# A hybrid encoder block on one core: the order of query splits, key splits, gate sums and refill steps

## The chip, the cores and the metric

The kernel runs on one core of a Trainium2 chip. The metric is the device time of one execution in microseconds (us), as the median of several executions. A profile of one execution shows every instruction of the core's engines: TensorE (PE, matmuls; PEld its weight loads), VectorE (DVE), ScalarE (ACT), GpSimd (POOL) and SyncE (SP, which here only issues DMA transfers). Each engine works through its own instructions in order, and an instruction that waits for another engine or for a transfer holds back everything behind it on its engine.

## What is computed

One encoder block on a sequence of 1024 rows of width 1024 with 16 learned rows put ahead, all in float32:

```python
u = _rms_norm(h, pre_w)
z = u @ w_in
rq, rk, rv, rg, aq, ak, av, ag, gr, ga = _split_in(z)
# branch A: two-way retention of rotary rq, rk with rv, 4 heads, chunks of 128
o_r = o_r * ret_nw * silu(rg)
y_r = o_r @ w_rb
# branch B: attention in a window of +-128 rows, 8 query heads in 2 groups,
# with the 16 learned rows always seen, and a sink in the softmax
o_a = o_a * silu(ag)
y_a = o_a @ w_ab
mix = sigmoid(gr) * y_r + sigmoid(ga) * y_a
return h + _rms_norm(mix @ w_o, post_w)
```

## The kernel before

**Numbers in two halves.** Every float32 operand of a large matmul is split into an upper part `h`, its value in the matmul's own format, and a lower part `l = x - h`. ACT (sometimes POOL) makes the upper part by a copy, and DVE the lower one by a subtraction (`dve_lo`, L92). A product is then three matmuls (`mm3`, L76 to L78): upper by upper, lower by upper, upper by lower. So nearly every operand passes through ACT and then DVE before PE can use it, and PE asks for the lower part one matmul after the upper one.

**Stages.** First the retention heads (to about 330 us), with projections run in between; then attention (about 330 to 549 us); then four phases of large products: `z` (the gates, from about 545 us), `r`, `a` (the two branches) and `o` (the output).

**Attention** (`attention`, from L1410) goes through 32 chunks, four pairs of heads with eight blocks of 128 queries. A chunk has three steps: `stage1` computes scores `ps` (PE), DVE adds the mask and takes the extremes (L1447, `raw`, `nm`), ACT takes exponentials (L1450); `stage2` transposes the scaled weights (PE, `pt`, L1483 to L1488) and splits them into `pah`/`pal`, `pbh`/`pbl` and `pm` (ACT, DVE); `stage3` multiplies with the values (PE, `po`). The banks of `pt` are used in turn, so PE can transpose for the next chunk only when DVE has read the last one. Between these steps PE does projections, in *steps* of three matmuls: `fill(n)` runs n steps. The table `BEGUN` (L1575 on) says which side tasks are written behind which step: fetching and splitting weights (`fetch_aq`, `half_w`), splitting queries (`split_q`, L670: ACT makes `aqh` in L678, DVE `aql`) and keys (`keys`, L717: ACT `kTh` in L724, DVE `kTl`), sums for later phases (`sum_row`, `pre_sum`, `pre_parts`). `hooked` (L848) ties each of these tasks behind the last exponential, row sum and softmax parts that were written ahead of it. Queries and keys are rotated in `rope_late` (L183): two DVE products (L187, L188), and two DMAs issued by POOL that add the turned halves (L192). The rotated tile can be split when these have landed.

**Start of attention.** `gen_av` (L903) projects the values, nine blocks; the last one's product `pav` is evacuated by ACT (`vah`, L917) and DVE (`val`, L918). Before the change this is done ahead of the first lines of `attention`; the first chunk's queries are split inside its own `stage1`.

**The phases.** Each phase is done in units `u` of seven products `p` of half-size blocks (a Strassen-like scheme), so that operands are sums and differences of blocks (`Phase.prepare`, L991). Units come in pairs: the order in phase `z` starts (0,1), (1,1), (0,3), (1,3), (0,2), (1,2), written as (unit, product). `run` prepares six products ahead (`LEAD = 6`). For the first two units of `z` (`early`) product 3 needs A12 - (A21 + A22 - A11), three DVE steps (L1025 to L1027) on tile `st`, then its split into `lhz` (ACT, L987) and `llz` (DVE). `Phase.split` notes its lower part in the list `ahead`: it always holds the lower part written last. Partial results gather in PSUM banks; `combine` (L1068) copies one to `u3` (ACT) and adds another to it (DVE, L1077), which frees that bank for the next product.

**Refills.** The right-hand blocks `B11`, `T1`, `B21`, `B22` lie in tiles `big`. While a phase ends, `refill` (L1154) writes the next phase's blocks into them: it loads pieces (SP), copies the upper part (ACT, L963) and subtracts the lower part (DVE, L92, `big<-a`). It gives each step a place counted from the phase's last product: -7 is seven products before. Phase `a`'s refill, for `o`, is the last and the shortest; its T blocks come ready made from DRAM.

**What sets the order.** The program's order is not the order of the queues. When the kernel is built, a planner with cost estimates of its own orders every engine's instructions by their place in the program and by when it expects their inputs. `tc.issue_after(i)`, and `follow(...)` around it, forbids one thing: instructions inside that run on the same engine as `i` may not be put ahead of `i`. They tie nothing on other engines.

Of the kernel before, what the change touches and what calls it, by code (L numbers as in the profile page):

```python
# [18 lines left out]
NB = SEQ // P  # L19
# [20 lines left out]
def block_kernel(ctx: ExitStack, tc: tile.TileContext, x0, xT, x, meta, w_in, w_rb, w_ab, w_out, post_w,  # L40
                 rope, tab, out):
    nc = tc.nc
# [232 lines left out]
    with tc.tile_pool(name="setup", bufs=1, reuse_waits="tile") as st:  # L275
# [61 lines left out]
        for k in range(KT):  # L337
            t = xr[k]
# [24 lines left out]
        split, wv0 = halves_w(U_V)  # L363
# [18 lines left out]
        first = [projT(wv0, 0, "pv0_0", vmeta0), projT(wv0, 1, "pv0_1"), projT(wv0, 2, "pv0_2")]  # L382
# [287 lines left out]
    def split_q(hp, e_, i):  # L670

        o = aq[hp][e_, i].rearrange("p (t q) -> p t q", q=64)
        if (hp, i) not in aqs:
            aqs[hp, i] = [aw.tile([P, 1024], R, tag=f"aq{t}", bufs=2, name=f"aq{t}{hp}_{i}") for t in "hl"], set()
            if len(aqs) == 1:
                aw.tile([P, 48], F32, name="space_aq")
        h, l = (t.rearrange("p (t e q) -> p t e q", e=2, q=64)[:, :, e_] for t in aqs[hp, i][0])
        nc.scalar.copy(h, o)  # L678
        dve_lo(l, o, h)
        aqs[hp, i][1].add(e_)  # L680


    def fetch_aq(hp):
# [219 lines left out]
    def gen_av():  # L903
        w = load_w(w_in, U_AV)
        for c in range(9):
            mt = None if c else vmt
            t = projT(w, c, f"pav{c}", mt)
            if c == 0:
                nc.scalar.activation(mt, mt, AF.Copy, scale=rcol[0:NM, 0:1])

                for r in range(4):
                    nc.vector.tensor_copy(vm[32 * r:32 * r + NM], mt)
                dve_lo(mt.bitcast(R), mt, vm[0:NM])
                for r in range(2):
                    nc.sync.dma_start(vm[32 * r + NM:32 * r + 2 * NM].bitcast(F32), mt)
            else:
                nc.scalar.activation(vah[:, c - 1], t[:, 0:256], AF.Copy, scale=rcol[:, c:c + 1])  # L917
                nc.vector.scalar_tensor_tensor(low_value(c - 1), t[:, 0:256], rcol[:, c:c + 1],  # L918
                                               vah[:, c - 1].bitcast(F32), op0=ALU.mult, op1=ALU.subtract)
            if NB - 3 < c < NB:  # L920
                yield


    av = gen_av()
# [41 lines left out]
    class Phase:  # L966
# [18 lines left out]
        def split(self, u, p, src):  # L985
            h, l = (lp.tile([P, 4, P], R, tag=t, bufs=LEAD, name=f"{t}{self.nm}{u}_{p}") for t in ("lh", "ll"))
            nc.scalar.copy(h, src)  # L987
            ahead[:] = [dve_lo(l, src, h)]
            self.ops[u, p] = h, l

        def prepare(self, u, p):  # L991
            if self.cur is not None and u // 2 != self.cur:
                self.raw = {}
            self.cur = u // 2
            g = nc.vector.tensor_tensor
            made = {1: 2, 6: 3}.get(p)
            if made not in self.pre.get(u, ()):
                made = None
            for q in (p, made):
                if self.fetch and q in POST and u not in self.early:  # L1000
                    self.fetch(u, *POST[q])
            if made:
                self.e[u, made] = gtile(f"e{u}{made}")
                nc.sync.dma_start(self.e[u, made], e_d[u, made])
            if p in (1, 2, 4):
                self.split(u, p, self.block(u, PROD[p][0]))
            elif p == 7:
                t = lp.tile([P, 4, P], F32, tag="st", bufs=3, name=f"st{self.nm}{u}S3")
                g(t, self.block(u, "A11"), self.block(u, "A21"), sub)
                self.split(u, 7, t)  # L1010
            elif p == 5:
                t = self.s[u] = lp.tile([P, 4, P], F32, tag="st", bufs=3, name=f"st{self.nm}{u}S")
                g(t, self.block(u, "A21"), self.block(u, "A22"), add)
                self.split(u, 5, t)
                g(t, t, self.block(u, "A11"), sub)
            elif p == 6:
                t = self.s[u]
                self.split(u, 6, t)
                if u in self.early or 3 in self.pre.get(u, ()):
                    del self.s[u]  # L1020
                else:
                    g(t, self.block(u, "A12"), t, sub)
            elif u in self.early:
                t = lp.tile([P, 4, P], F32, tag="st", bufs=3, name=f"st{self.nm}{u}S4")
                g(t, self.block(u, "A21"), self.block(u, "A22"), add)  # L1025
                g(t, t, self.block(u, "A11"), sub)
                g(t, self.block(u, "A12"), t, sub)  # L1027
                self.split(u, 3, t)
            else:
                self.split(u, 3, self.s.pop(u))  # L1030
# [123 lines left out]
    def refill(nm, src):  # L1154

        x = {}

        def load(i, j, ks=range(4)):
            def f():
                for k in ks:  # L1160
                    x[i, j, k] = t = stage(f"{nm}{i}{j}{k}", j)
                    src(t, 4 * i + k, j)
            return f

        def minus(o, a, b):
# [12 lines left out]
        def step(at, n, f):  # L1178
            for k, j in enumerate(n):
                at.setdefault(j, []).append(lambda k=k: f(k))  # L1180

        if nm == "a":
            at = {-16: [load(0, 0)], -14: [load(1, 1)]}
            each(at, -13, split("B11", 0, 0))
            at.update({-11: [got("T1")], -10: [load(1, 0)], -9: [got("T2")], -5: [got("T3")], -1: [got("T4")]})
            each(at, -7, split("B21", 1, 0))
            each(at, -3, split("B22", 1, 1))
            return at

        first = -21 if nm == "z" else -17  # L1190
        at = {first: [load(0, 0), load(0, 1)], -13: [load(1, 1)], -9: [load(1, 0, range(3))]}
        def behind(f):
            def g(k):
                with tc.issue_after(ahead[0]):
                    f(k)
            return g

        step(at, range(first + 2, first + 6), behind(minus((0, 1), (0, 1), (0, 0))))
        step(at, (-13, -12, -11, -10), split("B11", 0, 0))
        step(at, (-11, -10, -9, -8), split("T1", 0, 1))  # L1200
        step(at, (-9, -8, -7, -6), minus((0, 1), (1, 1), (0, 1)))
        step(at, (-7, -6, -5, -4), split("T2", 0, 1))
        step(at, (-5, -4, -3, -2), minus((0, 0), (0, 1), (0, 0)))
        step(at, (-3, -2, -1, 3), split("B21", 1, 0))
        step(at, (-1, 0, 1, 3), minus((0, 1), (1, 0), (0, 1)))
        at[0].append(load(1, 0, (3,)))
        step(at, (0, 1, 2, 4), behind(split("T3", 0, 0)))
        step(at, (4, 5, 6, 7), behind(split("B22", 1, 1)))
        step(at, (7, 8, 9, 10), behind(split("T4", 0, 1)))
        return at  # L1210
# [199 lines left out]
    def attention():  # L1410
# [123 lines left out]
                 gen_aq(3, 0), gen_aq(3, 1), pre]  # L1534
        fill = filler([hooked(works, BEGUN)])[0]

        with follow(*latest):
            fill(3)
        with follow(*latest):
            stage1(0, 0)  # L1540
        for k, (hp, n) in enumerate(chunks):
# [28 lines left out]
            if k in (12, 14, 21):  # L1570
# [13 lines left out]
             76: [(sum_row, 3, 1)], 79: [(sum_fetch, 4)], 82: [(split_q, 2, 0, 0)], 88: [(sum_row, 4, 0)],  # L1584
             89: [(sum_row, 4, 1)], 90: [(split_q, 2, 1, 0)], 92: [(sum_fetch, 5)], 100: [(sum_row, 5, 0)],
             101: [(sum_row, 5, 1)], 102: [(fetch_aq, 3)], 104: [(keys, 1, 1)], 105: [(sum_fetch, 6)],
             110: [(split_q, 2, 0, 1)], 116: [(keys, 1, 2)], 117: [(half_w, 'q', 3, 0)], 121: [(half_w, 'q', 3, 1)],
             122: [(pre_fetch, 9)], 123: [(sum_row, 6, 0)], 124: [(sum_row, 6, 1)], 126: [(split_q, 2, 1, 1)],
             127: [(sum_fetch, 7)], 133: [(pre_sum, 9, 0)], 134: [(pre_sum, 9, 1)], 136: [(keys, 1, 3)],
             139: [(pre_sum, 9, 2)], 140: [(pre_parts, 9)], 141: [(pre_fetch, 10)], 145: [(split_q, 3, 0, 0)],  # L1590
             146: [(sum_row, 7, 0)], 147: [(sum_row, 7, 1)], 150: [(split_q, 3, 1, 0)], 152: [(pre_sum, 10, 0)],
             153: [(pre_sum, 10, 1)], 155: [(pre_sum, 10, 2)], 157: [(pre_parts, 10)], 158: [(pre_fetch, 11)],
             164: [(split_q, 3, 0, 1)], 166: [(pre_sum, 11, 0)], 167: [(pre_sum, 11, 1)], 168: [(pre_sum, 11, 2)],
             170: [(pre_parts, 11)], 171: [(pre_fetch, 12)], 172: [(split_q, 3, 1, 1)], 176: [(pre_sum, 12, 0)],
             178: [(pre_sum, 12, 1)], 179: [(pre_sum, 12, 2)], 181: [(pre_parts, 12)], 182: [(pre_fetch, 13)],
             187: [(pre_sum, 13, 0)], 188: [(pre_sum, 13, 1)], 189: [(pre_sum, 13, 2)], 190: [(pre_parts, 13)]}

# [112 lines left out]
```

## Time and profile before

| | |
|---|---|
| median of 3 runs | 1034.35 us (1034.12 to 1037.31) |
| profiled execution | 1035.83 us |
| its span, first to last instruction | 1034.1 us |
| granted PE clock | 0.998 |
| instructions | 17322 |
| DMA | 188.45 MB, mean 182 GB/s |
| PE at work until / span | about 1027 / 1034.1 us |

The rows of the profile that the prediction shows are read thus. In the timeline, a row is one instruction: its start from the span's start, its length, engine, line, operation, the tile it writes and those it reads, shape, and in brackets the time that its engine stood idle before it and what ended that. Buffer numbers are left out of tile names. In the list of waits a row tells who waited for whom, the total in us, how often, and the longest. In the table of stretches, each row gives the stretch and its length, each engine's busy time in it, the granted clock, the share of time in which the DMA engines were busy, and GB/s.

### The profile page before, as it was taken

Reading aid. Unit: us, or ns where it says so; the run is one execution under the profiler, and the core shown is the slowest. Engines: PE = TensorE matmul, PEld = TensorE weight load, DVE = VectorE, ACT = ScalarE, POOL = GpSimd, SP = SyncE. Lnnn points to the kernel's source line nnn. Section 1 sums busy time; section 2 is a strip of 40 time slices with the busy share of each in tenths; the row PEclk is TensorE's granted clock in tenths of the full one; section 3 lists DMA queues with packets and bytes.
Section 4 is the critical chain, followed back from the end, with each engine's and each line's share of the span. In section 5 each row is a group of like instructions: output and inputs, shape, how many; then the busy total and the mean of one; then the engine's idle time right before and its main releaser. Section 6 shows DMA issues by size and latency. Waiting matters only on the chain. (4 is left out here: it accounts for less than half of the span.)

```text
span 1034.1 us, 17322 instructions
## 1 busy us (share of the span) xinstructions
PE 1022.3 (99%) x5883; PEld 898.8 (87%) x5883; DVE 831.9 (80%) x1802; ACT 502.0 (49%) x1129; POOL 226.3 (22%) x368
## 2 busy tenths in 40 slices
PE   9999999999999999999999999999999999999997
PEld 8998999989989888988888888888888888887886
DVE  7886759758876787777769999998989899777765
ACT  5531432523423466655667555455567456333442
POOL 3445244243341424443310000000000000110032
PEclk9999999999999999999999999999999999999999
DMA  9433123243241447666559589899874756889563
GB/s 360 164 87 88 63 46 87 76 78 112 80 97 62 103 152 206 184 183 174 154 171 347 178 287 330 312 319 319 276 265 141 257 196 200 246 216 330 139 122 81
DMA packets 98840, 188.45 MB, mean 182 GB/s; under 512 B 13024, under 2 KB 37632, under 8 KB 98192
## 3 DMA queue, kind: packets, MB, share of 16 engines
q1 hardware_dynamic: 81200, 162.89, 46.6%
q0 software_dynamic: 10176, 14.73, 9.5%
q10 hardware_dynamic: 7376, 9.73, 2.8%
q8 instruction: 46, 0.75, 0.3%
q14 instruction: 42, 0.34, 0.1%
HBM read 124.32 MB, written 57.68 MB: 176 GB/s over the span
## 5 line engine op out<-in xcount | busy, mean ns | idle before, releaser
L1310 POOL DMA_DIRECT2D mx_d<-c1a x4 | 3.6, 891 | 395.3 <-DMA a<-in_w_out_dram 368.6
L77 PE MATMUL bz<-big,llz 128*128 128x512 f32 x192 | 74.9, 390 | 0.5 <-DVE llz L92 0.5
L78 PE MATMUL bz<-big,lhz 128*128 128x512 f32 x192 | 74.4, 389 | 0.0
L76 PE MATMUL bz<-big,lhz 128*128 128x512 f32 x192 | 74.1, 389 | 0.0
L76 PE MATMUL pv<-wh,big 128*128 128x256 f32 x256 | 72.9, 285 | 0.0
L77 PE MATMUL pv<-wh,big 128*128 128x256 f32 x256 | 72.8, 284 | 0.0
L78 PE MATMUL pv<-wl,big 128*128 128x256 f32 x256 | 72.7, 284 | 0.0
L78 PE MATMUL bz<-T,lhz 128*128 128x512 f32 x176 | 68.5, 389 | 0.0
L77 PE MATMUL bz<-T,llz 128*128 128x512 f32 x176 | 68.5, 389 | 0.0
L76 PE MATMUL bz<-T,lhz 128*128 128x512 f32 x176 | 68.2, 389 | 0.0
L1450 ACT ACTIVATE p<-raw,nm 128x337 f32<-128x337 f32 (+1 forms) x64 | 35.5, 557 | 34.1 <-DVE nm L1447 30.5
L76 PE MATMUL paq<-big,wh 128*128 128x512 f32 x128 | 51.6, 403 | 0.0
L1463 POOL TENSOR_SCALAR p<-p,den 128x336 f32<-128x336 f32 (+2 forms) x60 | 32.6, 565 | 85.9 <-DVE den L1454 81.1
L78 PE MATMUL paq<-big,wh 128*128 128x512 f32 x128 | 50.2, 392 | 0.0
L77 PE MATMUL paq<-big,wl 128*128 128x512 f32 x128 | 50.2, 392 | 0.0
L76 PEld LDWEIGHTS pv<-wh,big 128*128 128x128 f32 x256 | 48.4, 189 | 0.4
L77 PEld LDWEIGHTS pv<-wh,big 128*128 128x128 f32 x256 | 48.3, 189 | 0.4
L78 PEld LDWEIGHTS pv<-wl,big 128*128 128x128 f32 x256 | 48.3, 189 | 0.3
L92 DVE TENSOR_TENSOR wl<-wr,wh 128x1024 fp32r<-128x1024 f32 x28 | 35.1, 1258 | 11.3 <-POOL wh L89 6.7
L77 PEld LDWEIGHTS bz<-big,llz 128*128 128x128 f32 x192 | 36.1, 188 | 8.1 <-DVE llz L92 0.8
L78 PEld LDWEIGHTS bz<-big,lhz 128*128 128x128 f32 x192 | 36.0, 188 | 7.5
L76 PEld LDWEIGHTS bz<-big,lhz 128*128 128x128 f32 x192 | 36.1, 188 | 7.5
(621 smaller groups left out, 3591.2 us busy)
## 6 DMA issues: line engine op xcount, KB each, us to landing
wrz<-in_w_in_dram SPq DMA_DIRECT2D x32, 512.0 KB, 6.0
wr<-in_w_in_dram SPq DMA_DIRECT2D x29, 512.0 KB, 4.0
we<-in_w_in_dram SPq DMA_DIRECT2D x16, 512.0 KB, 4.2
tg<-tg_d SPq DMA_DIRECT2D x32, 256.0 KB, 5.3
e<-e ACTq DMA_DIRECT2D x20, 256.0 KB, 2.4
e<-e SPq DMA_DIRECT2D x20, 256.0 KB, 4.6
xn<-in_x_dram SPq DMA_DIRECT2D x8, 512.0 KB, 9.4
oTr_d<-ost SPq DMA_DIRECT2D x16, 256.0 KB, 2.1
```

The costliest lines, as they stand in the source:

```text
L76: nc.tensor.matmul(o, ah, bh, start=first, stop=False, **kw)
L77: nc.tensor.matmul(o, al, bh, start=False, stop=False, **kw)
L78: latest[:] = [nc.tensor.matmul(o, ah, bl, start=False, stop=last, **kw).ins]
L92: return nc.vector.tensor_tensor(o, i, hi.bitcast(F32), ALU.subtract).ins
L1310: nc.gpsimd.dma_start(d, to, accum_op=ALU.add)
L1450: last["exp"] = nc.scalar.activation(pp[:, x_, w0 - o:w0 - o + 1 + wid], r[:, 0:1 + wid], AF.Exp, scale=-1.0, bias=nm_[:, x_:x_ + 1], accu ...
L1463: nc.gpsimd.tensor_scalar(v, v, den[:, x_:x_ + 1], 1.0, op0=ALU.mult, op1=ALU.mult)
```

## The change

Five parts:

1. `gen_av` yields once more, ahead of the evacuation of the last value block. `attention` then writes the two splits of the first queries (`split_q(0, 0, 0)` and `split_q(0, 1, 0)`) first, and lets the last evacuation follow, tied on ACT behind the two upper parts. `split_q` returns its ACT instruction for this.
2. `keys(1, 2)` moves from step 116 to step 120 of `BEGUN`.
3. `split_q(3, 1, 1)` moves from step 172 to step 169, which lies in the fill of the chunk before.
4. In the first two units of phase `z`, the first of the three sums for product 3 is tied behind the lower part written last (for unit 0 that of (1,1), for unit 1 that of (0,3)).
5. In phase `a`'s refill, the splits of B11, B21 and B22 are tied behind the lower part written last, as other refills already do for some of theirs. The definition of `behind` moves up for this.

```diff
@@ split_q
-        nc.scalar.copy(h, o)
+        upper = nc.scalar.copy(h, o).ins
         dve_lo(l, o, h)
         aqs[hp, i][1].add(e_)
+        return upper
@@ gen_av
             else:
+                if c == NB:
+                    yield
                 nc.scalar.activation(vah[:, c - 1], t[:, 0:256], AF.Copy, scale=rcol[:, c:c + 1])
@@ Phase.prepare
             elif u in self.early:
                 t = lp.tile([P, 4, P], F32, tag="st", bufs=3, name=f"st{self.nm}{u}S4")
-                g(t, self.block(u, "A21"), self.block(u, "A22"), add)
+                with tc.issue_after(ahead[0]):
+                    g(t, self.block(u, "A21"), self.block(u, "A22"), add)
                 g(t, t, self.block(u, "A11"), sub)
@@ refill
+        def behind(f):
+            def g(k):
+                with tc.issue_after(ahead[0]):
+                    f(k)
+            return g
+
         if nm == "a":
             at = {-16: [load(0, 0)], -14: [load(1, 1)]}
-            each(at, -13, split("B11", 0, 0))
+            each(at, -13, behind(split("B11", 0, 0)))
             at.update({-11: [got("T1")], -10: [load(1, 0)], -9: [got("T2")], -5: [got("T3")], -1: [got("T4")]})
-            each(at, -7, split("B21", 1, 0))
-            each(at, -3, split("B22", 1, 1))
+            each(at, -7, behind(split("B21", 1, 0)))
+            each(at, -3, behind(split("B22", 1, 1)))
             return at
@@ attention
         fill = filler([hooked(works, BEGUN)])[0]
 
+        with follow(*[split_q(0, e_, 0) for e_ in range(2)]):
+            next(av, None)
         with follow(*latest):
             fill(3)
@@ BEGUN
-             110: [(split_q, 2, 0, 1)], 116: [(keys, 1, 2)], 117: [(half_w, 'q', 3, 0)], 121: [(half_w, 'q', 3, 1)],
+             110: [(split_q, 2, 0, 1)], 117: [(half_w, 'q', 3, 0)], 120: [(keys, 1, 2)], 121: [(half_w, 'q', 3, 1)],
...
-             170: [(pre_parts, 11)], 171: [(pre_fetch, 12)], 172: [(split_q, 3, 1, 1)], 176: [(pre_sum, 12, 0)],
+             169: [(split_q, 3, 1, 1)],
+             170: [(pre_parts, 11)], 171: [(pre_fetch, 12)], 176: [(pre_sum, 12, 0)],
```

More of the change, by code (lines that the diff above doesn't have):

```diff
@@ L1180, in step @@
                 at.setdefault(j, []).append(lambda k=k: f(k))
-        if nm == "a":
-            at = {-16: [load(0, 0)], -14: [load(1, 1)]}
-            each(at, -13, split("B11", 0, 0))
-            at.update({-11: [got("T1")], -10: [load(1, 0)], -9: [got("T2")], -5: [got("T3")], -1: [got("T4")]})
-            each(at, -7, split("B21", 1, 0))
-            each(at, -3, split("B22", 1, 1))
-            return at
-        first = -21 if nm == "z" else -17
-        at = {first: [load(0, 0), load(0, 1)], -13: [load(1, 1)], -9: [load(1, 0, range(3))]}
         def behind(f):
@@ L1196, in behind @@
             return g
+        if nm == "a":
+            at = {-16: [load(0, 0)], -14: [load(1, 1)]}
+            each(at, -13, behind(split("B11", 0, 0)))
+            at.update({-11: [got("T1")], -10: [load(1, 0)], -9: [got("T2")], -5: [got("T3")], -1: [got("T4")]})
+            each(at, -7, behind(split("B21", 1, 0)))
+            each(at, -3, behind(split("B22", 1, 1)))
+            return at
+        first = -21 if nm == "z" else -17
+        at = {first: [load(0, 0), load(0, 1)], -13: [load(1, 1)], -9: [load(1, 0, range(3))]}
         step(at, range(first + 2, first + 6), behind(minus((0, 1), (0, 1), (0, 0))))
```

## The prediction

> **What bounds the kernel now.** I read the page first, then the waits of TensorE (PE), then the timeline of each engine around every wait.
>
> ```profile
> PE 1022.3 (99%) x5883; PEld 898.8 (87%) x5883; DVE 831.9 (80%) x1802; ACT 502.0 (49%) x1129; POOL 226.3 (22%) x368
> ```
>
> PE sets the end: 1022.3 of 1034.1 us, and the change takes no matmul away. It can only remove places where PE stands still. The waits of PE list them (total us, times, longest):
>
> ```profile
> PE ps L77 <- DVE aql L92: 1.0, 2, 0.5
> PE ba L76 <- DVE u3a L1077: 0.6, 1, 0.6
> PE pt L1483 <- DVE pal L92: 0.5, 1, 0.5
> PE bz L77 <- DVE llz L92: 0.5, 1, 0.5
> PE pt L1487 <- DVE pbl L92: 0.4, 1, 0.4
> ```
>
> These are six stops, all released by VectorE (DVE). Idle time understates them, because matmuls overlap. The PE timeline at the stop in stage a (start, length, idle):
>
> ```profile
> 941.35 0.39 PE L78 MATMUL ba<-big,lha 128*128 128x512 f32 x1
> 941.58 0.39 PE L76 MATMUL bo<-big,lho 128*128 128x512 f32 x1
> 942.52 0.51 PE L76 MATMUL ba<-big,lha 128*128 128x512 f32 x1 [0.56 <-DVE u3a L1077]
> 942.86 0.40 PE L77 MATMUL ba<-big,lla 128*128 128x512 f32 x1
> ```
>
> Matmuls start 0.23 apart (941.35, 941.58). The next was due at 941.81 and came at 942.52: 0.71 lost. The one behind it comes 0.34 later, not 0.23: 0.11 more. A stop thus costs its idle plus 0.16, plus 0.11 where a matmul of this kind follows. The six are worth about 0.77 + 0.77 (ps), 0.82 (ba), 0.64 (first pt), 0.71 (bz) and 0.58 (second pt): **4.3 us, 0.4% of the time, is the ceiling**. 0.3% (3.1 us) is about what a measurement of this kernel can tell from no change.
>
> **The change part by part.** No part adds or removes work. Each changes where a step stands in its engine's in-order queue, and DVE and ScalarE (ACT) carry the prices.
>
> *First queries' splits.* ACT, then DVE, then PE, where the first scores start:
>
> ```profile
> 329.92 0.47 ACT L917 ACTIVATE vah<-pav,rcol 128x256 fp32r<-128x256 f32 x1 [1.68 <-PE pav L78]
> 330.30 1.13 ACT L678 CAST aqh<-aq 128x512 fp32r<-128x512 f32 x2
> 330.43 0.48 DVE L918 SCALAR_TENSOR_TENSOR val<-pav,rcol,vah 128x256 fp32r<-128x256 f32 x1 [1.86 <-ACT vah L917]
> 331.96 0.68 DVE L92 TENSOR_TENSOR aql<-aq,aqh 128x512 fp32r<-128x512 f32 x1
> 332.70 0.39 PE L77 MATMUL ps<-kTh,aql 128*128 128x272 f32 x1 [0.51 <-DVE aql L92]
> ```
>
> ACT idles 1.68 us for the last value product, with both query casts (1.13) queued behind it. Placed ahead, they fit into that idle time, and DVE, idle 1.86, takes the two lower parts (2 x 0.68) there. The second ends near 330.4 in place of 332.64; PE wants it at 332.04. What is late next is only the last value, 0.1 to 0.3 later, which nobody reads for several blocks. Bounds: 0.77 saved; or nothing, and the last value 1.13 later, if the query tiles' memory is not free by then. I take -0.75.
>
> *Keys, 4 steps later.* The second block of `keys(1, 2)`:
>
> ```profile
> 451.99 0.41 ACT L724 CAST kTh<-akr 128x256 fp32r<-128x256 f32 x1 [1.69 <-DMA akr<-m_ak]
> 450.33 1.22 DVE L92 TENSOR_TENSOR wl<-wr,wh 128x1024 fp32r<-128x1024 f32 x1 [0.19 <-ACT wh L118]
> 452.43 0.42 DVE L92 TENSOR_TENSOR kTl<-akr,kTh 128x256 fp32r<-128x256 f32 x1 [0.88 <-ACT kTh L724]
> 452.87 0.69 DVE L187 TENSOR_TENSOR m_aq<-paq,sr 128x512 f32<-128x512 f32 x1
> 454.07 0.56 DVE L1447 CUSTOM_DVE_ANT_0 raw<-ps,mask,nsink 128x336 f32<-128x336 f32 x1
> 456.47 0.69 DVE L92 TENSOR_TENSOR pal<-pt,pah 128x512 fp32r<-128x512 f32 x1 [0.30 <-ACT pah L1493]
> 457.87 0.42 DVE L92 TENSOR_TENSOR pbl<-pt,pbh 128x256 fp32r<-128x256 f32 x1
> ```
>
> The key cast waits 1.69 for the rotation's DMA, and DVE stands 0.88 behind it, with two rotary products (1.20 from 452.87 to 454.07) and the scores' evacuation queued. Four steps later the split is written after those products. They then run from 451.55, the key's lower part after them, and the evacuation starts 0.88 earlier, as does the chain to `pal` (end 457.16 to 456.28) and `pbl` (458.29 to 457.41). PE wanted `pal` at 456.66: the first pt stop (0.64) goes, and the second shrinks by 0.24. The keys' own readers come well over a microsecond after 453.2. The rotation's two POOL-issued DMAs for the products start earlier too. Bounds: -0.88; or nothing, if the build's ordering leaves the key split in front. I take -0.85.
>
> *Third query split, 3 steps earlier.*
>
> ```profile
> 509.64 0.42 DVE L92 TENSOR_TENSOR pbl<-pt,pbh 128x256 fp32r<-128x256 f32 x1
> 511.43 1.05 ACT L823 CAST weh<-we 128x1024 fp32r<-128x1024 f32 x1 [0.92 <-DVE we L813]
> 515.77 0.42 DVE L92 TENSOR_TENSOR pbl<-pt,pbh 128x256 fp32r<-128x256 f32 x1
> 516.12 0.68 DVE L92 TENSOR_TENSOR aql<-aq,aqh 128x512 fp32r<-128x512 f32 x1
> ```
>
> The split is tied behind the last softmax parts of its block, so it follows `pbl` at 515.77 and ends at 516.80, 0.68 after PE wants it. Three steps earlier it belongs to the block before and is tied behind the `pbl` of 509.64. ACT has 0.92 idle there for the 0.62 cast. DVE's 0.60 then delays one evacuation and one lower part that PE wants microseconds later. I take -0.77; the other end, +0.3, is that evacuation's chain becoming late.
>
> *First gate sums.* Each of the first two units forms A21+A22-A11 and A12 minus that (L1025, L1026, L1027):
>
> ```profile
> 544.32 0.69 DVE L1025 TENSOR_TENSOR stz0S<-wrz,wrz 128x512 f32<-128x512 f32 x1 [3.66 <-DMA wrz<-in_w_in_dram]
> 545.04 0.69 DVE L1026 TENSOR_TENSOR stz0S<-stz0S,wrz 128x512 f32<-128x512 f32 x1
> 545.65 0.68 DVE L92 TENSOR_TENSOR llz<-wrz,lhz 128x512 fp32r<-128x512 f32 x1
> 544.51 0.62 ACT L987 CAST lhz<-wrz 128x512 fp32r<-128x512 f32 x1
> 549.40 0.68 DVE L1025 TENSOR_TENSOR stz1S<-wrz,wrz 128x512 f32<-128x512 f32 x1
> 554.82 0.68 DVE L92 TENSOR_TENSOR llz<-stz1S,lhz 128x512 fp32r<-128x512 f32 x1
> 556.00 0.39 PE L77 MATMUL bz<-big,llz 128*128 128x512 f32 x1
> ```
>
> Two sums stand before the lower part that PE waits for. Behind it, `llz` starts when its cast ends, 545.16 instead of 545.65: 0.49 of the 0.71 goes, 0.1 to 0.2 stays. But unit 0's sums now also wait for the second `llz` (unit 1), and unit 1's first sum for unit 0's third lower part. By my count that part ends at 550.8 (three sums and a cast of 0.62 after about 547.6), so unit 1's chain starts 1.4 later than 549.40. Its lower part ended at 555.50, 0.5 before PE read it (556.00, which also comes 0.5 earlier now). Without the six foreign steps that DVE ran inside that chain (3.6) it ends near 554.0 and PE waits for nothing; with all of them near 556.9, a new stop of 1.4. Bounds: -0.7 to +0.9; I take -0.2.
>
> By the Trainium skill (VectorE: DVE Perf Modes, "The DRAIN you can't avoid") a semaphore between vector instructions costs nothing extra, so a chain of sums would cost only its lengths. The trace differs: the dependent pair above starts 0.72 apart, independent ones 0.61 (941.18 and 941.79 below). By the page the chain would end 0.2 to 0.3 earlier; the sum goes by the rows.
>
> *Last refill.* DVE before the stop in stage a:
>
> ```profile
> 935.76 0.69 DVE L1009 TENSOR_TENSOR sto1S<-wro 128x512 f32<-128x512 f32 x1 [4.18 <-DMA wro<-mx_d]
> 937.58 1.89 DVE L92 TENSOR_TENSOR big<-a,big 128x512 fp32r<-128x512 f32 x3
> 941.18 0.68 DVE L1301 SCALAR_TENSOR_TENSOR c1a<-tg,c1a 128x512 f32<-128x512 f32 x1
> 941.79 0.68 DVE L1077 TENSOR_TENSOR u3a<-u3a,ba 128x512 f32<-128x512 f32 x1
> ```
>
> DVE was held 4.18 us by one load, and ten steps queued; `u3a`, whose end frees PE's accumulator, is the last. Four of the ten are B21 lower parts. The tie puts two of these behind the lower part of the stage's last product. If they fall behind `u3a` as well, it ends at 941.26 and the whole 0.82 goes; if they only change places with that lower part, nothing does. The order between is the build's, not the program's: I take half, -0.4. The added ties hold only DVE steps; the casts on ACT stay, B11's last stage tile is freed about 2 us later, and so is one load on SP's queue, whose data is read much later.
>
> **The sum**: -0.75 - 0.85 - 0.77 - 0.2 - 0.4 = -2.97. The profiled execution took 1035.83 (its span 1034.1 and 1.7 around it), 1.48 above the median of the runs, 1034.35, and would become 1032.9; I take the difference from the median: **1031.4**.
>
> **The rivals.**
>
> 1. *Everything goes* (both bounds in the z and a stages reached): -0.75 - 0.88 - 0.77 - 0.7 - 0.82 = -3.9, **1030.4**. For it: each part touches one of the six stops. Against: the serial sums.
>
> 2. *The change does not do what it says.* Ties and step numbers only bound an order that the build chooses; the key split and the two refill parts may stay in front, and the sums may pay back what they save. Then only the two query splits count: -1.5, **1032.8**.
>
> 3. *Loads hold the end.*
>
> ```profile
> 550.00:560.00 10.00, 10.00 (x46) 8.21 (x46) 10.00 (x18) 9.22 (x18) 0.00 (x0) 1.00 1.05 388
> 930.00:940.00 10.00, 10.00 (x46) 8.27 (x45) 4.93 (x10) 5.52 (x10) 0.88 (x1) 1.00 0.96 364
> ```
>
> The last two columns are the DMA share and GB/s: full. If the load that held DVE until 935.76 lands when it did, PE only reaches the stop earlier and waits longer: what the first four parts won (2.6) is given back, leaving about the refill's 0.4: **1034.0**. Against it: the loads are issued behind DVE and PE events, which all move. The Trainium skill (DMA: Bandwidth & Descriptors, "Where 436 GB/s comes from") puts the HBM side at about 358 GB/s a core, by which these rows are at the limit and this rival would hold; the trace shows 388, above it.
>
> 4. *Slower: the serial sums on a full DVE.* DVE has no idle time in the first of these stretches (10.00 of 10.00). The tie leaves it empty for 0.84 more at the start, and twice for a cast (0.7 each): 2.2. If that comes on top of all the foreign steps, unit 1's lower part ends at 559.1 and PE, which wants it at 555.5, stops 3.6 where it stopped 0.7: +2.9. It outweighs the rest (-1.5 to -2.8) from about 558.3 on: **1035.3**, more if later lower parts follow late.
>
> **How the numbers follow.** Forecast 0.44 (1030.9 to 1032.1); rival 1 0.17; 2 0.21; 3 0.07; 4 0.11. Below 1031.25 lie rival 1 and four tenths of the forecast: 0.35. Above 1037.45 lies half of rival 4: 0.06. The rest, 0.59, is within 0.3%. The range, 1030.2 to 1035.0, leaves out a little below and about 0.1 above.
>
> **What would show it.** Among PE's waits: no `ps` behind `aql`; at most one short `pt` behind `pbl`; `bz` behind `llz` near 0.1. DVE's 0.88 before `kTl` is gone, rotary products in front. The first `llz` stands ahead of L1025. `u3a` starts before 941 less the shift. I am wrong if PE waits for `llz<-stz1S` for over a microsecond, if `u3a` still has four `big` steps in front, or if new waits appear that no part touches, from an order that the build chose anew.

## The result and the profile after

The changed kernel takes 1045.27 us (median of 6, 1043.09 to 1045.87) beside 1035.22 us of the kernel before (median of 6, 1034.12 to 1037.31): a ratio of 1.009, 95% interval 1.0074 to 1.0106. (This ratio and those further down are worked out over all runs; the quotient of the two medians is 1.0097.) It is 0.9% slower, or 10 us by the medians. The profiled execution took 1045.71 us, with a span of 1043.9. The line numbers of the changed kernel lie 1 to 4 above those of before.

The waits of PE in the changed kernel (total us, times, longest):

```profile
PE bz L76 <- ACT lhz L990: 2.9, 1, 2.9
PE bz L77 <- DVE llz L92: 1.8, 3, 1.1
...
PE pt L1487 <- DVE pal L92: 1.1, 1, 1.1
PE pe L77 <- DVE wel L92: 0.8, 1, 0.8
```

Both stops behind `aql` are gone, and `ba` behind `u3a` is not among the long ones in this execution. In their place PE waits longest in stage z, first for a cast of ACT and then for DVE. The windows of the changed kernel over that place (PE, PEld, DVE, ACT, POOL busy; granted clock; DMA share; GB/s):

```profile
555.00:560.00 5.00, 2.07 (x9) 1.15 (x7) 5.00 (x9) 4.03 (x8) 0.00 (x0) 1.00 1.06 399
560.00:562.50 2.50, 1.34 (x3) 0.71 (x4) 2.50 (x6) 2.50 (x6) 0.00 (x0) 0.69 1.05 374
562.50:567.50 5.00, 5.00 (x13) 3.84 (x13) 5.00 (x10) 3.11 (x6) 0.00 (x0) 0.50 0.85 303
```

Two losses stand here, one behind the other. From 556 to 562 PE starts only three matmuls. Then it is fully busy, and for 5 us its granted clock is 0.50: 13 matmuls in 5.00 us, where the kernel before has 24 in each of these stretches of 5 us. The timeline of PE shows both:

```profile
556.03 0.40 PE L78 MATMUL bz<-big,lhz 128*128 128x512 f32 x1
559.34 1.54 PE L76 MATMUL bz<-big,lhz 128*128 128x512 f32 x3 [2.91 <-ACT lhz L990]
562.02 0.79 PE L77 MATMUL bz<-big,llz 128*128 128x512 f32 x1 [1.14 <-DVE llz L92]
562.62 0.63 PE L78 MATMUL bz<-big,lhz 128*128 128x512 f32 x1
```

Counted by starts, as in the prediction (0.23 is the pitch), the matmul at 559.34 is 3.1 late, the three in it stand 0.3 too far apart each (0.6 together), the next one is 1.4 late, and from 562.02 on 13 matmuls stand 0.43 apart or a little more, 2.8 in all. With 0.8 at 552 to 553 that is 8.7, less the 0.5 that the first gate stop lost: 8.2 of the 9.8 us between the two spans. Why the cast was late is on the timelines of DVE and ACT in the changed kernel:

```profile
547.68 0.69 DVE L92 TENSOR_TENSOR llz<-wrz,lhz 128x512 fp32r<-128x512 f32 x1
...
549.74 0.69 DVE L1031 TENSOR_TENSOR stz0S<-wrz,stz0S 128x512 f32<-128x512 f32 x1
551.53 0.69 DVE L92 TENSOR_TENSOR big<-xT,big 128x512 fp32r<-128x512 f32 x1 [1.10 <-ACT big L966]
552.85 0.69 DVE L92 TENSOR_TENSOR llz<-stz0S,lhz 128x512 fp32r<-128x512 f32 x1 [0.62 <-ACT lhz L990]
553.46 0.68 DVE L1029 TENSOR_TENSOR stz1S<-wrz,wrz 128x512 f32<-128x512 f32 x1
...
557.67 0.69 DVE L1031 TENSOR_TENSOR stz1S<-wrz,stz1S 128x512 f32<-128x512 f32 x1
558.27 3.10 DVE L92 TENSOR_TENSOR T<-xT,T 128x512 fp32r<-128x512 f32 x5
561.28 0.69 DVE L92 TENSOR_TENSOR llz<-stz1S,lhz 128x512 fp32r<-128x512 f32 x1
```

```profile
550.88 0.62 ACT L966 CAST big<-xT 128x512 fp32r<-128x512 f32 x1 [0.36 <-DMA xT<-xs]
551.74 0.42 ACTq L1530 DMA_DIRECT2D oTa_d<-oa  x1
552.20 0.62 ACT L990 CAST lhz<-stz0S 128x512 fp32r<-128x512 f32 x1 [0.70 <-DMA xT<-xs]
...
556.59 2.18 ACT L966 CAST T<-xT 128x512 fp32r<-128x512 f32 x4 [0.28 <-DMA xT<-xs]
558.67 0.61 ACT L990 CAST lhz<-stz1S 128x512 fp32r<-128x512 f32 x1
```

In the kernel before, unit 0's cast stood ahead of all these rows:

```profile
546.97 0.63 ACT L987 CAST lhz<-stz0S 128x512 fp32r<-128x512 f32 x1
```

Now unit 0's sums are ready at 550.43 and its cast starts at 552.20. The cast stands on ACT behind a refill cast that waits for its load and behind the issue of a store. Unit 1's sums are tied behind unit 0's lower part and so begin at 553.46, and up to unit 1's lower part, which ends at 561.97, the build put eight refill steps (three `big`, five `T`) and two foreign sums (steps of other products) into that chain on DVE; one more `big` stands ahead of unit 0's part. The prediction had 554.0 to 556.9, and 559.1 for its slow rival.

### The profile page after: what moved, and what is told of

It reads as the page before. It is cut to its first block, busy times and chain, and to the rows that moved or that the text cites. A ratio compares the mean times of both kernels' runs of the same rounds, so it can differ in the third digit from the quotient of the medians.

```text
span 1043.9 us, 17316 instructions
## 1 busy us (share of the span) xinstructions
PE 1027.0 (98%) x5883; PEld 899.8 (86%) x5883; DVE 832.4 (80%) x1802; ACT 502.8 (48%) x1129; POOL 227.4 (22%) x368
## 5 line engine op out<-in xcount | busy, mean ns | idle before, releaser
L76 PE MATMUL bz<-big,lhz 128*128 128x512 f32 x192 | 75.8, 397 | 3.0 <-ACT lhz L990 2.9
L78 PE MATMUL bz<-big,lhz 128*128 128x512 f32 x192 | 75.1, 394 | 0.0
```

Of the source, the lines that this page charges most:

```text
L76: nc.tensor.matmul(o, ah, bh, start=first, stop=False, **kw)
L78: latest[:] = [nc.tensor.matmul(o, ah, bl, start=False, stop=last, **kw).ins]
```

## The experiments

**Theory A:** the tie of the first gate sums is the whole loss: it makes a chain over two units, and PE's standing still brings down its clock. **Rival B:** the build chose a new order everywhere, and the tie is only one part of it. Later experiments ask what makes the chain late (A3 the refill's steps inside it, A4 the waits in series by themselves, A5 the store on ACT's queue), and what became of the other parts' gains (C, D). Medians in us, each beside runs of the kernel before on the same chip:

| run | this | before | ratio | 95% interval |
|---|---|---|---|---|
| e1 change without the gate tie | 1035.88 | 1035.95 | 0.9998 | 0.9990 to 1.0006 |
| e2 gate tie alone | 1044.74 | 1035.95 | 1.0087 | 1.0073 to 1.0100 |
| e3 change, 12 extra matmuls | 1043.24 | 1035.95 | 1.0070 | 1.0057 to 1.0083 |
| e4 both units tied behind the first lower part | 1040.27 | 1035.95 | 1.0039 | 1.0026 to 1.0052 |
| e5 change, refill's lower parts behind the chain | 1039.35 | 1035.58 | 1.0039 | 1.0025 to 1.0053 |
| e6 first splits, third split 6 steps earlier | 1035.58 | 1035.58 | 1.0000 | 0.9991 to 1.0009 |
| e7 first splits alone | 1035.14 | 1035.58 | 0.9995 | 0.9986 to 1.0004 |
| e8 third split alone | 1036.71 | 1035.58 | 1.0010 | 1.0001 to 1.0019 |
| e9 as e5, its casts too | 1045.66 | 1035.89 | 1.0083 | 1.0058 to 1.0108 |
| e10 change, 20 extra matmuls | 1043.34 | 1035.89 | 1.0070 | 1.0050 to 1.0090 |
| e11 first splits, second sums tied | 1035.34 | 1035.89 | 0.9995 | 0.9986 to 1.0004 |
| e12 as e9, store on POOL | 1041.64 | 1035.46 | 1.0053 | 1.0033 to 1.0073 |
| e13 change, store on POOL | 1043.01 | 1035.46 | 1.0073 | 1.0054 to 1.0091 |

**e1 and e2: the tie taken out, and the tie alone.**

```diff
                 t = lp.tile([P, 4, P], F32, tag="st", bufs=3, name=f"st{self.nm}{u}S4")
-                with tc.issue_after(ahead[0]):
-                    g(t, self.block(u, "A21"), self.block(u, "A22"), add)
+                g(t, self.block(u, "A21"), self.block(u, "A22"), add)
```

> The changed kernel with the tie of the first gate sums taken out again; the other four parts stay. Theory A (the serial sums of the two first gate units are the whole loss): the stops behind lhz and llz at 552 to 561 us and the stretch at half clock vanish, PE's first gate stop is back at about 0.7, and the time falls by 8 to 10 us, to 1034 to 1036.5, that is within 0.2% of the kernel before. Theory B (the build chose a new order everywhere, the tie is only a part of it): at least half of the loss stays, over 1040.

> The kernel before with the tie of the first gate sums alone. Theory A: the same stops (3 us behind lhz of unit 1, 1.4 after it) and the same stretch at half clock; 8 to 10 us slower than before, 1043 to 1046. Theory B: under 5 us slower.

The waits of PE, first without the tie, then with the tie alone:

```profile
PE pe L77 <- DVE wel L92: 1.3, 2, 0.8
...
PE bz L77 <- DVE llz L92: 0.6, 1, 0.6
```

```profile
PE bz L76 <- ACT lhz L987: 3.2, 1, 3.2
PE bz L77 <- DVE llz L92: 1.6, 3, 0.9
```

Without the tie the first gate stop is back (0.6), the long waits and the fall of the clock are gone, and the time is that of before. With the tie alone the stops, the half clock and the loss (8.8 us) are all there. Theory A holds, B falls. The first list also says something of the other four parts: with both `aql` stops gone (1.5 by starts) the kernel is no faster than before.

**e3 and e10: more work for PE.** Extra matmuls ahead of unit 1's third product, whose result its first real matmul overwrites (20 in e10):

```diff
             t = st[at][0]
+            if (self.nm, u, p) == ("z", 1, 3):
+                for _ in range(12):
+                    nc.tensor.matmul(t, self.prev[0], self.prev[1], start=True, stop=True)
             h, l = self.ops.pop((u, p))
```

> The changed kernel with twelve extra matmuls on PE ahead of the third product of gate unit 1; their result is overwritten, and every output is as before. They take 2.7 us at full clock and lie where PE stood idle (3.1 + 0.7 us). Theory A1 (the clock fell to 0.5 because PE stood still for most of 5 us): the granted clock stays at 1.0 from 560 to 568, the 2.9 us of half clock are not lost, and the kernel is 2 to 3 us faster than the changed one in spite of more work, about 1042.5. Rival A2 (the clock fell for another reason, such as the transfers or a load step): the clock still falls, and the time is 1045 or more.

> The changed kernel with twenty extra matmuls (4.5 us at full clock) where twelve stood; outputs as before. Twelve left PE idle for 1.2 us and sparse for 3, and the clock fell for 3.4 us in place of 6.8. Theory A1 (idleness alone): PE is now idle for less than 1.5 us in all, the granted clock stays 1.0 throughout from 550 to 570; the time is 0 to 1.3 below that with twelve, 1041.5 to 1043. Rival A2: the clock falls again at 559 to 562.

In e3 all twelve ran at 550.9 to 553.8, and in e10 eighteen at 552.9 to 557.1: most of them not in the stop at unit 1, but ahead of it, so that PE reached it later and stood still for less. The windows of 1 us, in which the clock falls and comes back: of the changed kernel, then of e3, then of e10 at its emptiest place:

```profile
560.00:561.00 1.00, 0.87 (x2) 0.23 (x2) 1.00 (x3) 1.00 (x3) 0.00 (x0) 0.97 1.08 375
561.00:562.00 1.00, 0.00 (x0) 0.00 (x0) 1.00 (x3) 1.00 (x3) 0.00 (x0) 0.50 1.04 377
...
567.00:568.00 1.00, 1.00 (x5) 0.76 (x4) 1.00 (x3) 0.52 (x1) 0.00 (x0) 0.62 0.99 332
```

```profile
559.00:560.00 1.00, 0.37 (x1) 0.37 (x2) 1.00 (x2) 1.00 (x3) 0.00 (x0) 0.53 1.07 391
...
562.00:563.00 1.00, 1.00 (x5) 0.81 (x4) 1.00 (x2) 0.98 (x2) 0.00 (x0) 0.76 1.05 385
```

```profile
560.00:561.00 1.00, 0.75 (x4) 0.29 (x2) 1.00 (x3) 1.00 (x3) 0.00 (x0) 1.00 1.08 389
561.00:562.00 1.00, 0.47 (x2) 0.43 (x3) 1.00 (x3) 1.00 (x4) 0.00 (x0) 1.00 1.03 379
```

A mean of 0.97 in a stretch of 1 us means that the clock fell 0.06 before its end, at 560.94; a mean of 0.62 that it came back at 567.76. So the changed kernel ran at half clock for 6.82 us, e3 from 559.06 to 562.48, 3.42 us: two windows and one of the same length, 3.41. With twelve extra matmuls, then, the clock still fell, where I had 1.0 throughout. With twenty extra matmuls PE stands still for 0.8 us only, and the clock stays at 1.00. The transfers are as dense in all three (375, 391 and 389 GB/s in the first row of each), so A2 falls: the clock goes by how little PE did. In time, twelve matmuls brought the ratio from 1.0090 to 1.0070 though they add work, some 2 us as I had said (2 to 3), with intervals that overlap. Twenty bring no more (1043.34, where I had 1041.5 to 1043); their own 4.5 us, then in the way, are the likely reason, but no run shows it.

**e4: the tie on the first lower part only.** `ahead[0]` in the tie becomes unit 0's first lower part, kept aside when it is written:

```diff
-                with tc.issue_after(ahead[0]):
+                with tc.issue_after(self.lows[0, 1]):
```

> The kernel before with the sums of both first units tied behind the first lower part alone (unit 0's), not behind the latest one. One foreign sum instead of a chain of waits stands between. Theory A (it is the chain of lower part, sums, cast, lower part that is too long): the first gate stop falls from 0.7 to 0.1 or 0.2, the lower part of unit 0's sum comes near 552.5 where PE wants it at 552.4 to 552.9, so a stop of up to 0.5 there, unit 1's comes at 555, in time, the clock does not fall; in all -0.6 to +0.5, so 1034.5 to 1035.7 beside 1035.2. Theory B (any tie here makes the build order the stage badly): 3 us slower or more.

I was wrong here: I had 1034.5 to 1035.7, and the kernel is about 4 us slower than before (2.7 to 5.4). The clock stayed at 1.0, but PE was 1.2 late at 552 and 1.6 at 758 by starts, both times for `lhz`. ACT at the first place:

```profile
551.70 0.62 ACT L963 CAST big<-xT 128x512 fp32r<-128x512 f32 x1 [0.42 <-DMA xT<-xs]
552.44 0.38 ACTq L1528 DMA_DIRECT2D oTa_d<-oa  x1
552.86 0.62 ACT L987 CAST lhz<-stz0S 128x512 fp32r<-128x512 f32 x1 [0.54 <-DMA xT<-xs]
```

This tie makes no long chain over both units, and still unit 0's cast has moved behind the refill and the store, as in the change. I had put its lower part near 552.5; its cast alone ends at 553.48. So the length of the chain on DVE is not enough as a cause, which led to the next runs.

**e5 and e9: the refill's steps tied behind the chain,** on DVE alone, then on ACT too:

```diff
-    get_sum("T1")
+    with tc.issue_after(ahead[0]):
+        get_sum("T1")
```

In e9 the second line reads `with follow(ahead[0], cast[0]):`, where `cast` holds the last cast of a gate part.

> The changed kernel, and in it the first refill of the gate stage (T1: four casts on ACT and four lower parts on DVE, each waiting for a load) tied behind the chain of the two first units. Theory A3 (the chain itself fits; the refill's steps that the build put inside it, with their loads, make it late): the lower part of unit 1's sum ends near 556.0 in place of 561.97, PE's stop there is 0.5 or less in place of 3.1 + 1.4, the clock does not fall, and the time is 1036 to 1038.5. Rival A4 (the added waits in series are too long by themselves, whatever stands between): a stop of 2 us or more stays at unit 1, and the time is over 1041.

> As the run with the first refill tied behind the chain, and now its four casts on ACT also stand behind the chain's casts (there they stayed in front, and unit 0's cast of its sum waited 0.6 for a refill's load, at 550.86). Theory A3 (foreign steps and their loads make the chain late): unit 0's lower part comes at 550.2 in place of 551.5, unit 1's near 554.8, PE's stop there (1.16 + 0.3) falls below 0.2, and the time is 1.0 to 1.6 us less than with the lower parts tied alone, 1037.5 to 1038.5, unless the later refill is then late for the fifth product. Rival A4 (the waits in series are too long by themselves): the stop at unit 1 stays over 1.0.

In e5 the stop at unit 1 shrank from 3.1 + 1.4 to 1.2 + 0.3 by starts, the clock did not fall, and over 5 us came back (1.0090 to 1.0039): the refill's steps inside the chain are most of the loss. But a stop stayed, and the time, 1039.35, is above the 1036 to 1038.5 that A3 had. e9, which takes the refill's casts away as well, did not remove the stop (1.1 + 0.3, the sign of rival A4). Its timeline of ACT says why:

```profile
550.98 0.37 ACT L1527 COPY oa<-po 128x256 f32<-128x256 f32 x1 [0.24 <-PE po L1522]
552.68 0.38 ACTq L1530 DMA_DIRECT2D oTa_d<-oa  x1
553.10 0.62 ACT L990 CAST lhz<-stz0S 128x512 fp32r<-128x512 f32 x1 [1.75 <-DMA xT<-xs]
```

No cast of the refill is left ahead of unit 0's cast, and still ACT stands 1.75 us, released by a load of the refill. What stands there is the issue of the attention's last store. In the compiled program this store waits for two things: ACT's own copy, and the DMA semaphore that the refill's second load counts on as well. While ACT waits to issue the store, everything behind it on ACT waits too. In e9 PE then waits 1.8 us for an `llz` at 574, behind the refill's late steps on DVE, and its time is no better than the change's, where I had 1037.5 to 1038.5.

**e12 and e13: the store issued by POOL,** which is idle in this stage; in e9's kernel, and in the change as it is:

```diff
             if n % 2:
-                nc.scalar.dma_start(
+                (nc.gpsimd if (hp, n) == (3, 7) else nc.scalar).dma_start(
```

> As the run with the refill's casts and lower parts both tied behind the chain, with one edit: the last store of the attention's output is issued by POOL's queue, not by ACT's. There ACT stood 1.75 us at this store's issue (to 552.68, released by a load of the refill on the same queue's semaphore), and unit 0's cast of its sum stood behind it, ready since 551.28. Theory A5 (the store's issue holds ACT's queue, and so the chain): that cast starts within 0.2 of the end of the sums, the lower parts of both units come 1.6 to 1.8 us earlier, PE's stops at 553 and 557 (0.75 + 1.5) go to 0.3 or less together; the time falls by 1.5 to 3 us against that run, unless its late T part (2.0 at 572) takes it back. Rival A4 (the sums in series are too long by themselves): the stop at unit 1 stays over 1.0.

> The whole change as it is, with one edit: the last store of the attention's output is issued by POOL's queue, not by ACT's. Theory A5: unit 0's cast of its sum is no longer behind the store; the build then also puts unit 1's cast in front of the refill's later casts; stops of 0.2 to 1.2 in all at 552 to 557 in place of 5.7, no fall of the clock, and 1035.5 to 1037.5 beside 1035.9, 8 us less than the change. Rival A4: over 1041, with a stop of 2 us or more at unit 1.

The chain in e12, DVE with unit 0's cast on ACT beside it:

```profile
547.63 0.69 DVE L1031 TENSOR_TENSOR stz0S<-wrz,stz0S 128x512 f32<-128x512 f32 x1
549.00 0.69 DVE L92 TENSOR_TENSOR llz<-stz0S,lhz 128x512 fp32r<-128x512 f32 x1 [0.69 <-ACT lhz L990]
...
553.52 0.69 DVE L92 TENSOR_TENSOR llz<-stz1S,lhz 128x512 fp32r<-128x512 f32 x1 [0.69 <-ACT lhz L990]
```

```profile
548.35 0.62 ACT L990 CAST lhz<-stz0S 128x512 fp32r<-128x512 f32 x1
```

The cast starts when the sums end (548.32). Both stops together are 0.5 by starts, where e9 had 2.2 (I had 0.3 or less): A5 holds and A4 falls, the sums in series fit by themselves. In e13 the store is gone from the chain, but four refill steps on DVE are still in it (one ahead of unit 0's part, three ahead of unit 1's), and PE's stop at unit 1 is 2.5 by starts, with the clock at 1.0. Taken alone, e13 bears the signs that I had given to rival A4 (over 1041, a stop of 2 or more); it is e12, where no refill step stands in the chain, that rules A4 out. The store and the refill's steps are thus seen apart. My times were wrong, though: e13 came to 1043.0 where I had 1035.5 to 1037.5. e12 is 4.0 below e9 by the medians (3.1 by the ratios, where I had 1.5 to 3), but at 1041.6 still 6 above the kernel before (its profiled execution, at 1037.83, is the fastest of four). In e12 the put-off refill stops PE for 2.0 at 568. In e13 there are stops of 0.5 to 1.1 at 640, 761 and 795, at steps that the edit does not name. Such stops stand in other traces too, also in that of e8, whose stage z has the compiled order of before. How much of e12's and e13's rest is theirs stays open, as each kernel was profiled in one execution. The mean granted clock is on record for every execution: it is 0.994 to 0.998 in e9, 0.997 to 0.999 in e12 and 0.996 to 0.999 in e13, beside 0.997 to 0.999 for the kernel before and 0.995 to 0.996 for the change. A stretch of 6.82 us at half clock lowers this mean by 0.003, so in some executions of e9 and e13 the clock seems to have fallen too, where no profile shows it.

**e6, e7, e8: the splits alone.** e7 has the first queries' splits (the hunks of `split_q`, `gen_av` and `attention`), e8 the third split at step 169, e6 the first splits and the third split at step 166:

```diff
-             164: [(split_q, 3, 0, 1)], 166: [(pre_sum, 11, 0)], 167: [(pre_sum, 11, 1)], 168: [(pre_sum, 11, 2)],
-             170: [(pre_parts, 11)], 171: [(pre_fetch, 12)], 172: [(split_q, 3, 1, 1)], 176: [(pre_sum, 12, 0)],
+             164: [(split_q, 3, 0, 1)], 166: [(split_q, 3, 1, 1), (pre_sum, 11, 0)], 167: [(pre_sum, 11, 1)], 168: [(pre_sum, 11, 2)],
+             170: [(pre_parts, 11)], 171: [(pre_fetch, 12)], 176: [(pre_sum, 12, 0)],
```

> The kernel before with the first queries' splits moved ahead and the third query split moved by 6 steps in place of 3, so that its lower part stands behind the pbl of the block before and no longer between the two sums of the same unit. Theory C (at three steps the lower part delays the second sum by 0.6, and with it the parts, the next load and DVE, which waits for that load): sums, parts and the next load come 0.5 to 0.6 earlier, PE's stops behind wel (1.0 and 0.7 without the gate tie) shrink to 0.3 to 0.9 in all, and the time is 0.5 to 1.3 us below before. Rival D (the load lands at its own time, whatever is issued before): the stops behind wel stay at 1.3 or more, and the time is that of before within 0.4.

> The kernel before with the first queries' splits ahead alone. The forecast of this part: PE's stop behind aql at 332 (0.77) goes and nothing takes its place, 0.7 to 0.8 less, 1035.2 beside 1035.95. Rival D: it is given back at the next place where PE's chain hangs on a load (the keys at 456, the gate parts at 525); the stops there are longer by as much, and the time is that of before.

> The kernel before with the third query split 3 steps earlier alone. The forecast of this part: 0.77 less. Theory C: the stop behind aql at 516 goes (0.79), and stops behind wel of 0.7 to 1.0 at 525 take its place, because the second sum and the next load come 0.6 later; the time is within 0.4 of before. Rival D: no new stop behind wel with this part alone, since PE arrives there late enough.

The gate parts that PE waits for at 525, on DVE in e8, then in e7, then in e6:

```profile
510.75 0.69 DVE L92 TENSOR_TENSOR aql<-aq,aqh 128x512 fp32r<-128x512 f32 x1
511.35 0.69 DVE L813 TENSOR_TENSOR we<-we 128x512 f32<-128x512 f32 x1
...
513.15 1.23 DVE L92 TENSOR_TENSOR wel<-we,weh 128x1024 fp32r<-128x1024 f32 x1
...
518.11 0.69 DVE L813 TENSOR_TENSOR we<-we,we 128x512 f32<-128x512 f32 x1 [1.53 <-DMA we<-in_w_in_dram]
```

```profile
511.96 1.23 DVE L92 TENSOR_TENSOR wel<-we,weh 128x1024 fp32r<-128x1024 f32 x1
516.87 0.69 DVE L814 TENSOR_TENSOR we<-we,we 128x512 f32<-128x512 f32 x1 [0.63 <-DMA we<-in_w_in_dram]
524.42 1.23 DVE L92 TENSOR_TENSOR wel<-we,weh 128x1024 fp32r<-128x1024 f32 x1
```

```profile
511.70 1.23 DVE L92 TENSOR_TENSOR wel<-we,weh 128x1024 fp32r<-128x1024 f32 x1
516.77 0.69 DVE L814 TENSOR_TENSOR we<-we,we 128x512 f32<-128x512 f32 x1 [1.39 <-DMA we<-in_w_in_dram]
524.32 1.22 DVE L92 TENSOR_TENSOR wel<-we,weh 128x1024 fp32r<-128x1024 f32 x1 [0.63 <-ACT weh L824]
```

In all three DVE gets the next `we` 4.9 to 5.1 after `wel` starts, and the next `wel` comes 7.55 after that. The load goes into buffers that the parts before it have read (in e6 and e8 SP's queue waits 2.6 for `wel` before it issues one), so this is a loop through a load, and it keeps its own pace. With the first splits alone (e7) PE reaches it late enough and does not wait, because it still loses 0.7 at 515 behind `aql`. Once that stop is taken away (e6), `wel` comes at the same time as in e7 within 0.1, and PE waits 0.8 for it, 1.0 by starts: the gain is given back 10 us later. At three steps (e8) the query's lower part also stands between two sums of the same unit (510.75), the second sum is 0.6 later, and PE waits for `wel` in two places, 1.5 by starts. So C is right for that 0.6, and D for the rest; neither alone. e7 is 0.4 us below before, e8 1.1 above, e6 even; of these only e8's interval leaves out 1, and only just. C had e6 0.5 to 1.3 below and e8 within 0.4, so it has both times wrong; D has e6's time right, but had no new stop in e8. That e8's 1.1 is the split's is not shown: its profiled execution, the slowest of ten, has stops of 1.6 at 758 and 1.0 at 792 in stage z, whose order the split does not change.

**e11: a version meant to beat both.** The first splits, and of the gate sums only the second, tied behind the first lower part:

```diff
                 g(t, self.block(u, "A21"), self.block(u, "A22"), add)
-                g(t, t, self.block(u, "A11"), sub)
+                with tc.issue_after(self.lows[0, 1]):
+                    g(t, t, self.block(u, "A11"), sub)
```

> A candidate to beat the kernel before: the first queries' splits ahead, and of the gate sums only the second one of each of the two first units (minus A11) tied behind the first lower part; the first sum stays in front. By the rows of before the lower part can start when its cast ends, 0.49 earlier than behind two sums, and the chain of unit 1 is put off by one step, 0.6, inside the 0.5 to 0.8 that it had to spare. Theory A (only the length of the chain matters): the gate stop falls from 0.7 to 0.1 or 0.2 and no stop of over 0.3 comes at 552 to 558; with the first splits -1.0 to -1.4, 1034.3 beside 1035.6. Theory B (any tie makes the build reorder the stage): new stops of 1 us or more, 1036 or more.

All that is left in PE's waits of 0.3 or more, past the start:

```profile
PE ps L77 <- DVE aql L92: 0.6, 1, 0.6
PE pt L1492 <- DVE pbl L92: 0.4, 1, 0.4
```

The gate stop is gone without a new one, as theory A said; by starts 0.3 at 554.87 is the largest in its place. The time, 0.5 us below before (1.4 below to 0.4 above, where I had 1.0 to 1.4 below), cannot be told from no change. It is the lowest ratio of all, with e7, but no proof of a gain.

## Why the prediction was wrong

The forecast was 1031.4 us, in a range of 1030.2 to 1035.0; the slow rival had 1035.3. It came to 1045.27.

- **First gate sums** (-0.2, bounds -0.7 to +0.9) is the step that failed; it measured about +8.2 in the trace and +8.8 alone. The half on the first stop was right: `llz` stands ahead of the sums and the stop fell from 0.7 to 0.26 by starts. What failed is the sentence that unit 0's third lower part "ends at 550.8 (three sums and a cast of 0.62 after about 547.6)". It counted the sums on DVE and let the cast run as soon as they end. But the cast had moved on ACT too, from 546.97 to behind a refill cast and a store whose issue waits for a load; it started 1.8 after the sums were ready, and the part ended at 553.54. From there unit 1's chain took ten foreign steps into it, where I had counted six. Rival 4 named the mechanism and the place, with a price of 2.9: it too had only DVE's queue in it, and no clock.
- **The clock** is in no part of the prediction. Of the 8.2, 2.8 is the half clock. By the Trainium skill (TensorE: Matmul & The Clock Gate, "What's actually happening") the clock is halved after an idle window of about 3.4 us and restored after a busy one; the traces agree with the length (3.42 us in e3, 6.82 in the change), but three matmuls ran in the window ahead of the change's fall. By that rule a stop forecast at over 3 us, as in rival 4, would have needed this term.
- **First queries' splits** (-0.75): the stop is gone in each of the runs that have it. The time alone, -0.4 (-1.4 to +0.4), agrees, and nothing more can be said at this size.
- **Keys, 4 steps later** (-0.85): nothing. The compiled instruction lists of all five engines are the same row for row with and without this edit, alone and in the whole change: my lower bound, "the build's ordering leaves the key split in front". DVE's idle time ahead of `kTl` stayed (0.88 before, 1.48 in the change). The wait behind `pal`, 0.5 before and 1.1 after, is no effect of it either: in e3, the same program up to there, it is not among PE's long waits, and DVE has no listed idle time ahead of `kTl`. What differs is when the rotation's transfer lands in that execution.
- **Third query split** (-0.77): the stop is gone, and 1.0 to 2.0 came in its place behind `wel`. That is rival 3, in a place that I had not named.
- **Last refill** (-0.4): the lower end, nothing. The tie does change DVE's order: two of the four `big` steps now stand behind the lower part of the last product. But all four still stand ahead of `u3a`, which starts at 951.66 in the change; they only changed places with that lower part, now at 949.25:

```profile
947.45 1.29 DVE L92 TENSOR_TENSOR big<-a,big 128x512 fp32r<-128x512 f32 x2
...
949.85 1.29 DVE L92 TENSOR_TENSOR big<-a,big 128x512 fp32r<-128x512 f32 x2
```

PE's wait behind `u3a` is none to 1.4 in the eight traces with the tie (none in the change, 1.4 in e12) and none to 1.1 in the seven without. In all fifteen it is what DVE's idle time for the load at the head of that queue has above 3.6 (the list has no wait under 0.2): 4.18 gave 0.6 before, 5.03 gave 1.4 in e12, 4.76 gave 1.1 in e7, which lacks the tie, 3.77 gave none in the change. So the landing of the load sets this stop, and the tie does not. I read one execution's 0.6 as a constant.

Of the signs that I had named, three came true: PE waits for `llz<-stz1S` over a microsecond (1.14, after 2.91 for its cast), `u3a` still has four `big` steps in front, and there are new waits that no part touches.

## What to carry to other kernels

A tie on one engine moves the whole chain that hangs on it: for each step that moves, list what it now stands behind on every queue, ACT's DMA issues among them, and ask what those wait for. Where PE is 98 or 99% busy, a stop that a loop over a load sets can come back when PE is made faster (in e6 10 us later), so look for the next landing before a gain is counted. A stop seen in one execution next to a load is a sample, and should be read in a second trace before it becomes a term of a sum.

## What the hardware showed that I had not expected

- The clock fell though PE was not quite idle: in the 3.41 us ahead of the fall (to 560.94) the change started three matmuls where some 15 fit; in e3 (fall at 559.06) it was five. In the next window PE was idle for its first 1.1 us and the clock stayed at half; in e3, with 0.6 idle at the start of its half window, it came back after one. Where between these the clock decides is not shown.
- A stop of 2.5 us (e13) or of 1.2 + 0.5 (e4) left the clock at 1.0 in the profiled executions.
- A DMA issue on ACT's queue held that engine for up to 1.75 us (e9), waiting for a load that SP had issued. Moving this one issue to POOL took 1.7 us of PE's stops at 553 and 557 away (e9 to e12).
